# A Conformer and attention trunk on one core: two more channel blocks of the depthwise convolution on VectorE, pointwise weights' lower parts by accumulating DMA, GpSimd's arithmetic on other engines, and zero-padded lower rotary keys

## The chip, the cores and the metric

The kernel runs on one core of one Trainium2 chip. The metric is the device time of one execution in microseconds (us). A program is timed in several runs, and the median is given. One more execution is recorded by the hardware profiler; its span runs from the first instruction to the last one.

The core has five instruction queues: TensorE (PE, with its weight loads shown as PEld), VectorE (DVE), ScalarE (ACT), GpSimd (POOL) and SyncE (SP), which here only starts DMAs. POOL also starts DMAs, those that add into their destination.

## What is computed

Two layers of a trunk over 512 tokens with 1024 channels. Cut to what matters here:

```python
def conformer_conv(h, w_pw1, b_pw1, w_dw, b_dw, ln_g, ln_b, w_pw2, b_pw2):
    u = h @ w_pw1 + b_pw1
    a, gate = jnp.split(u, 2, axis=-1)
    u = a * jax.nn.sigmoid(gate)
    u = jnp.pad(u, ((0, 0), (CONV_WIDTH - 1, 0), (0, 0)))
    u = lax.conv_general_dilated(u, w_dw[:, None, :], ...) + b_dw
    u = jax.nn.silu(layer_norm(u, ln_g, ln_b))
    return u @ w_pw2 + b_pw2
...
        sc = (jnp.einsum('bqhd,bkhd->bhqk', qn, k_nope, ...)
              + jnp.einsum('bqhr,bkr->bhqk', qr, k_rope, ...)) * scale
...
def squared_relu_mlp(h, w1, w2):
    return jnp.square(jax.nn.relu(h @ w1)) @ w2
```

Layer 0 is the convolution module (31 taps for each channel) and a squared-ReLU MLP of width 4096. Layer 1 is attention with 8 heads, whose scores are the sum of a 128-wide product and a 64-wide rotary product that shares one key over all heads, and a second MLP.

## The kernel before, in words

Channels lie on the 128 partitions, tokens on the free axis, so each of the 8 channel blocks is a tile of 128 x 512. Every float32 product is made of three matmuls in a second 32-bit format (fp32r): each operand is split into an upper part (rounded to that format) and a lower part (what is left), and upper x upper, lower x upper and upper x lower are added in PSUM (`products_of`). A weight block of 128 x 1024 takes 24 matmuls.

**Weights** (`weight`). A block is loaded by SP into one of 3 `raw` buffers and split into one of 6 pairs `wh`, `wl`. For the blocks of the MLP (`ff1`, `ff2`) ACT writes the negated upper part into `wl` and the upper part into `wh`, and POOL starts a DMA that adds the block from memory onto `wl`. For all others ACT writes `wh` and DVE or POOL subtracts, whichever the planner takes (`VG`).

**The convolution module.** For each channel block c, pw1's blocks c and 8+c give the two halves; DVE multiplies each by the row norms (`za`, `zg`), ACT takes the sigmoid, DVE multiplies to `u`. The 31 taps are then done in one of two ways, given by a letter of `CONV`:

- V: `taps_vector`. ACT makes the first two taps, DVE the other 29, each one SCALAR_TENSOR_TENSOR of 128 x 482 to 510, into two accumulators, and adds these.
- T: `taps_tensor`. `u` is dealt through memory into one of three tiles `uu` (SP: one DMA `dealt<-big`, four `uu<-dealt`), nine weight tiles of 128 x 512 come from `cw`, and TensorE does 36 plain float32 matmuls of 128 x 128, whose results ACT (DVE for the last block) writes back in 16 pieces or more. `TAPS_AFTER` says behind which pw1 product a block's taps stand.

Before, two blocks are V and six are T. The layer norm over channels follows: an estimate of the mean (`K`, from blocks 0 and 1) is subtracted, sums and squares are added up, TensorE sums over partitions, and each block is normalised, put through SiLU and split for pw2.

**The MLP.** After each ff1 product, `z` = relu times norm on DVE, upper part of the square on ACT, the full square on POOL, their difference on DVE.

**Attention.** `scores` adds five matmuls into PSUM for each head and block of 128 queries. The fifth multiplies 64 rows only: `qr[rs]` with the lower half of the rotary key, `KR[1][rs]`.

**The order.** Nothing is issued where it stands in the code. All operations are recorded, and a planner (`Program`) with a cost for each kind of operation puts them into one order for each engine, chooses between VectorE and GpSimd where two ways are given (`binary`), gives out the buffers, and fills stretches where it expects TensorE to idle ahead of a new PSUM tile with matmuls on the identity that nothing reads (`mm<-ident`; 8 of them are 16 records of the trace). At run time each engine keeps that order and waits on semaphores. All instructions are therefore issued by one line of the code, line 556, and the trace is read by tiles, not by lines.

Of the kernel before, what the change touches and what calls it, by code (L numbers as in the profile page):

```python
# [15 lines left out]
T = 512  # L16
# [47 lines left out]

GAINS = {"dq": "mix_pre1", "dkv": "kvin_g", "kr": "kvin_g"}
# [40 lines left out]
CONV = "VTVTTTTT"  # L106
# [8 lines left out]
TAPS_AFTER = {1: 3, 3: 5, 4: 6, 5: 7, 6: 7}  # L115
# [112 lines left out]
class Program:  # L228
# [89 lines left out]
    def arrival(self, op, end, state):  # L318

        if "dma" not in op.method:  # L320
            return end
        n = max(_size(self.model(v)) for v in list(op.args) + list(op.kwargs.values()) if isinstance(v, View))
        state[0] = max(state[0], end + 650) + n * 1.42
        return state[0] + 850
# [235 lines left out]
def trunk(ctx: ExitStack, tc: tile.TileContext, xT, wts, vec, rope, cw, out):  # L560
# [25 lines left out]
    def pair():  # L586
        return big(F32R), big(F32R)
# [38 lines left out]
    def weight(key):  # L626

        while BLK[key] not in blocks:
            i = len(blocks)
            n = _cols[i]  # L630
            raw, hi, lo = nc.tile(RAW), nc.tile(WH, F32R), nc.tile(WL, F32R)
            step = 256 if i < 2 else n
            for o in range(0, n, step):
                nc.sync.dma_start(out=raw[:, o : o + step], in_=wts[i, :, o : o + step])
            if _names[i][0] in GAINS:
                for k in range(KT):
                    split_scaled(raw, v(GAINS[_names[i][0]], k), k * P, P, (hi, lo))
# [12 lines left out]
        return blocks[BLK[key]]  # L650
# [121 lines left out]
    def feed_forward(layer, X, r, F):  # L772

        for q in range(4):
# [4 lines left out]
            for m, (t0, n) in order:  # L779
# [8 lines left out]
                nc.gpsimd.tensor_tensor(out=zz[:, s], in0=z[:, s], in1=z[:, s], op=ALU.mult)  # L788
# [16 lines left out]
    def post_norm_groups(gen, F, on_half, g=None):  # L805
# [26 lines left out]
    for k in range(KT):  # L832
        a = (acc, part)[k % 2]
        sq = a if k < 2 else tmp()
        if k % 2:
            nc.scalar.activation(sq, h[k], AF.Square)
        else:
            nc.gpsimd.tensor_tensor(out=sq, in0=h[k], in1=h[k], op=ALU.mult)
        if k > 1:
            (nc.gpsimd, nc.vector)[k % 2].tensor_tensor(out=a, in0=a, in1=sq, op=ALU.add)  # L840
# [127 lines left out]
    for n, c in enumerate(LN_ORDER[:-1]):  # L968
        nc.vector.tensor_tensor(out=CO[c], in0=CO[c], in1=K, op=ALU.subtract)
        add_square(acc, CO[c], slice(0, T), n == 0, "gpsimd")  # L970
        if n == 0:
            xs = CO[c]
        else:
            xt = xs if n > 1 else big()
            nc.gpsimd.tensor_tensor(out=xt, in0=xs, in1=CO[c], op=ALU.add)
# [5 lines left out]
    for t0, n in (HA, HB):  # L981
# [13 lines left out]
        for c in range(KT):  # L995
            nc.binary(VG, out=CO[c][:, s], in0=CO[c][:, s], in1=dln[:, s], op=ALU.subtract)
# [57 lines left out]
    KR = pair()  # L1054
# [51 lines left out]
    for t in (HA, HB):  # L1106
# [3 lines left out]
        split(rotate(products(("kr",), XH, *t), t[1], s, r1), s, KR)  # L1110
# [39 lines left out]
    def scores(hd, half):  # L1150

        rs = slice(64 * (hd % 2), 64 * (hd % 2) + 64)
        PN[hd, half] = []
        kn, qn, qr = KN[hd], QN[hd], QR[hd]
        for i in (2 * half, 2 * half + 1):
# [5 lines left out]
            seq += [(qr[:, qs], KR[0][:, ks]), (qr[rs, qs], KR[1][rs, ks])]  # L1161
# [193 lines left out]
```

## Time and profile before

| | |
|---|---|
| median of 3 runs | 1167.62 us (1165.93 to 1168.73) |
| the profiled execution's own time | 1166.24 us |
| its span | 1164.5 us |
| TensorE busy | 1127.0 us, 97% of the span |
| ScalarE, VectorE, GpSimd busy | 621.3, 491.0, 400.7 us |
| mean granted TensorE clock | 0.994 |

How to read it: in a row of the timeline the first number is the start, the second the duration of the row's instructions together, both in us; a bracket at the end gives the idle time of that engine ahead of the row and what ended it. In a row of the stretches the numbers are the length, then the busy time of each engine with its count of instructions, the granted clock (PEclk), the mean busy share of the 16 DMA engines, and GB/s. A plain float32 matmul or filler has two records in the trace.

The stages, by the start of their first matmul: pw1 with the convolution from the start to 155.5 us, layer norm to 171.5, pw2 and the norms to about 250, the first MLP to 560, latent projections and norms to 660, attention to 780, output projection to 820, the second MLP to 1140, the end.

### The profile page before, as it was taken

The page shows a single profiled execution, that of the slowest core. Times are in us where ns is not written, and L with a number is a line of the kernel's source. Part 1 is how long each engine was busy: PE and PEld are TensorE (multiplying, and loading weights), DVE is VectorE, ACT ScalarE, POOL GpSimd, SP SyncE. Part 2 cuts the span into 40 slices and gives each one's busy share as a digit, 9 for nine tenths or more (in the row PEclk, how much of TensorE's full clock was granted, in tenths as well). Part 3 has the DMA queues.
Part 4 walks back from the last instruction along what each step waited for, and adds up shares of the span by engine and source line. Part 5 has one row for each costly group of instructions (what it writes and reads, how often), then busy time and mean ns, then how long its engine had stood idle before and what let it go on. Part 6 is the DMA issues. An engine that isn't in the chain of part 4 may idle for free.

```text
span 1164.5 us, 16571 instructions
## 1 busy us (share of the span) xinstructions
PE 1127.0 (97%) x6094; PEld 963.9 (83%) x6094; DVE 491.0 (42%) x1042; ACT 621.3 (53%) x1288; POOL 400.7 (34%) x423
## 2 busy tenths in 40 slices
PE   8998979999999999999989999999999999999997
PEld 6787979988888888888988877798888888888886
DVE  6898364671021121122698877428400211211215
ACT  4464748765544444454465867547644544444441
POOL 5573444452132132133333435145512312322322
PEclk9999989999999999999999999999999999999999
DMA  9556411669888888889210213245988987988842
GB/s 333 185 202 230 142 37 33 164 156 245 199 183 192 193 193 188 197 188 210 69 38 30 68 40 91 73 121 133 242 194 188 195 194 187 191 197 188 189 80 73
DMA packets 62865, 181.91 MB, mean 156 GB/s; under 512 B 7104, under 2 KB 15936, under 8 KB 62784
## 3 DMA queue, kind: packets, MB, share of 16 engines
q0 software_dynamic: 18432, 67.12, 34.2%
q1 hardware_dynamic: 43200, 112.69, 28.2%
q8 instruction: 48, 0.79, 0.3%
q10 hardware_dynamic: 1152, 1.05, 0.3%
q14 instruction: 33, 0.27, 0.1%
HBM read 177.15 MB, written 3.67 MB: 155 GB/s over the span
## 4 chain that ended last, share of the span: by engine, by line
PE 85%; DVE 9%; ACT 3%; issue 1%; DMA 0%; SPq 0%; POOL 0%; DVEq 0%
PE mm L556 82%; DVE big L556 5%; PE bc L556 3%; ACT big L556 3%; DVE tmp L556 2%; DVE stat L556 1%; DVE wl L556 1%; DMA h<-xT 0%; ACT tmp L556 0%; SPq L556 0%; DVE h L556 0%; ACT wh L556 0%; POOL h L556 0%; ACT wl L556 0%; DVEq L1351 0%
## 5 line engine op out<-in xcount | busy, mean ns | idle before, releaser
L556 PE MATMUL mm<-big,wh 128*128 128x512 f32 (+1 forms) x3304 | 897.9, 358 | 11.5 <-DVE big L556 9.1
L556 PEld LDWEIGHTS mm<-big,wh 128*128 128x128 f32 x3304 | 585.7, 189 | 108.7 <-DVE big L556 14.4
L556 PE MATMUL mm<-big,wl 128*128 128x512 f32 (+1 forms) x1652 | 586.1, 357 | 3.8 <-DVE wl L556 3.7
L556 PEld LDWEIGHTS mm<-big,wl 128*128 128x128 f32 x1652 | 311.5, 189 | 50.3 <-DVE wl L556 5.1
L556 ACT ACTIVATE wl<-raw 128x512 fp32r<-128x512 f32 x256 | 147.7, 624 | 321.7 <-issue 288.9
L556 ACT ACTIVATE wh<-raw 128x512 fp32r<-128x512 f32 (+2 forms) x348 | 196.1, 605 | 35.6 <-DMA raw<-wts 17.7
L556 POOL DMA_DIRECT2D wl<-wts x128 | 111.2, 869 | 284.0 <-ACT wl L556 268.7
L556 DVE TENSOR_TENSOR big<-mm,big 128x512 f32<-128x512 f32 (+3 forms) x102 | 60.6, 599 | 206.2 <-PE mm L556 191.7
L556 DVE SCALAR_TENSOR_TENSOR tmp<-mm,big 128x512 f32<-128x512 f32 (+1 forms) x72 | 44.8, 630 | 241.6 <-PE mm L556 240.6
L556 POOL TENSOR_TENSOR tmp<-tmp 128x512 f32<-128x512 f32 (+1 forms) x72 | 69.8, 972 | 195.2 <-DVE tmp L556 190.1
L556 POOL TENSOR_TENSOR wl<-raw,wh 128x512 fp32r<-128x512 f32 (+2 forms) x67 | 91.0, 1377 | 96.7 <-ACT wh L556 88.4
L556 DVE TENSOR_TENSOR big<-tmp,big 128x512 fp32r<-128x512 f32 (+1 forms) x86 | 54.4, 639 | 87.2 <-POOL tmp L556 43.7
L556 ACT ACTIVATE big<-mm 128x512 fp32r<-128x512 f32 (+5 forms) x102 | 51.1, 504 | 44.6 <-PE mm L556 43.8
L556 POOL TENSOR_TENSOR big<-big,tmp 128x256 f32<-128x256 f32 (+1 forms) x40 | 42.6, 1066 | 60.6 <-ACT tmp L556 56.6
L556 POOL TENSOR_TENSOR h<-h,tmp 128x256 f32<-128x256 f32 x56 | 44.0, 846 | 47.8 <-DVE tmp L556 47.8
L556 POOL TENSOR_TENSOR big<-big,big 128x256 f32<-128x256 f32 (+2 forms) x34 | 37.6, 1109 | 64.7 <-ACT big L556 38.4
L556 DVE SCALAR_TENSOR_TENSOR big<-big,vt,big 128x510 f32<-128x510 f32 (+28 forms) x58 | 57.7, 1050 | 0.0
L556 PE MATMUL mm<-big,big 128*128 128x256 f32 (+7 forms) x256 | 56.1, 344 | 0.0
L556 ACT ACTIVATE big<-mm,vt 32x128 f32<-32x128 f32 (+1 forms) x96 | 46.2, 482 | 13.6 <-PE mm L556 12.5
L556 DVE TENSOR_TENSOR big<-big,tmp 128x256 f32<-128x256 f32 (+1 forms) x65 | 36.2, 560 | 37.1 <-ACT tmp L556 24.5
L556 PEld LDWEIGHTS mm<-big,big 128*128 128x128 f32 (+1 forms) x256 | 39.6, 188 | 12.9 <-issue 7.8
L556 PEld LDWEIGHTS mm<-uu,big 128*128 128x128 f32 x432 | 48.8, 192 | 0.3
(78 smaller groups left out, 706.7 us busy)
## 6 DMA issues: line engine op xcount, KB each, us to landing
raw<-wts SPq DMA_DIRECT2D x164, 512.0 KB, 6.1
wl<-wts POOLq DMA_DIRECT2D x128, 512.0 KB, 6.7
big<-cw SPq DMA_DIRECT2D x54, 256.0 KB, 5.0
raw<-wts SPq DMA_DIRECT2D x12, 192.0 KB, 2.3
h<-xT SPq DMA_DIRECT2D x8, 256.0 KB, 4.5
raw<-wts SPq DMA_DIRECT2D x16, 128.0 KB, 2.6
dealt<-big SPq DMA_DIRECT2D x6, 256.0 KB, 2.1
uu<-dealt SPq DMA_DIRECT2D x24, 64.0 KB, 3.3
```

The costliest lines, as they stand in the source:

```text
L556: return f(*args, **kwargs)
```

## The change

- `CONV` becomes `VVTVTVTT`: blocks 0, 1, 3 and 5 on VectorE, 2, 4, 6 and 7 on TensorE; `TAPS_AFTER` follows.
- `weight`: pw1 and pw2 blocks from the fifth on get their lower part like the MLP's, by ACT and an accumulating DMA; the first four, and `dq` and the like as before, by VectorE alone. The weights of attention keep the choice of two engines.
- GpSimd's element-wise work in the start, the layer norm, the sums of squares and the MLP's square goes to VectorE or ScalarE. The residual additions, the rotary rotation and the splits of attention's weights stay.
- The lower part of the rotary key becomes two tiles of 128 rows, one for even and one for odd heads, with zeros in the other half, so that the fifth matmul of `scores` has 128 rows.
- The planner's model gives an accumulating DMA 2.03 times the time of a plain one.

```diff
-CONV = "VTVTTTTT"
+CONV = "VVTVTVTT"
...
-TAPS_AFTER = {1: 3, 3: 5, 4: 6, 5: 7, 6: 7}
+TAPS_AFTER = {2: 4, 4: 6, 6: 7}
...
+        slow = 2.03 if "accum_op" in op.kwargs else 1.0
+        state[0] = max(state[0], end + 650) + n * 1.42 * slow
+        return state[0] + 850 * slow
...
-            elif _names[i][0] in ("ff1", "ff2"):
+            elif i >= 4 and _names[i][0] in LO_BY_DMA:
...
-                engines = VG
+                engines = VG if _names[i][0] in ATT else ("vector",)
...
-                nc.gpsimd.tensor_tensor(out=zz[:, s], in0=z[:, s], in1=z[:, s], op=ALU.mult)
+                nc.scalar.activation(zz[:, s], z[:, s], AF.Square)
...
-                add_square(accs[0], F[m], s, m == 0, "gpsimd" if m < 6 else "vector")
+                add_square(accs[0], F[m], s, m == 0, "vector")
...
-        if k % 2:
-            nc.scalar.activation(sq, h[k], AF.Square)
-        else:
-            nc.gpsimd.tensor_tensor(out=sq, in0=h[k], in1=h[k], op=ALU.mult)
+        nc.scalar.activation(sq, h[k], AF.Square)
...
-            nc.binary(VG, out=CO[c][:, s], in0=CO[c][:, s], in1=dln[:, s], op=ALU.subtract)
+            nc.binary(("vector",), out=CO[c][:, s], in0=CO[c][:, s], in1=dln[:, s], op=ALU.subtract)
...
-        split(rotate(products(("kr",), XH, *t), t[1], s, r1), s, KR)
+        kr = rotate(products(("kr",), XH, *t), t[1], s, r1)
+        nc.scalar.activation(KR[:, s], kr[:, s], AF.Copy)
+        for j in range(2):
+            rows = slice(64 * j, 64 * j + 64)
+            nc.vector.tensor_tensor(
+                out=KL[j][rows, s], in0=kr[rows, s], in1=KR[rows, s].bitcast(F32), op=ALU.subtract
+            )
...
-            seq += [(qr[:, qs], KR[0][:, ks]), (qr[rs, qs], KR[1][rs, ks])]
+            seq += [(qr[:, qs], KR[:, ks]), (qr[:, qs], KL[hd % 2][:, ks])]
```

The planner makes new orders of all this. Counted over the whole program, TensorE's taps go from 216 matmuls to 144, its fillers from 28 to 96, GpSimd's element-wise operations from 278 to 108, its DMAs from 128 to 148, VectorE's taps from 58 to 116, ScalarE's instructions from 1266 to 1354 and SP's DMAs of `cw` from 54 to 36.

TensorE at the end of pw1, before: the last matmul of pw1 (`wh15` is the sixteenth block's upper part) and what follows it. `uu00` is the dealt tile of block 5, and two more T blocks follow it.

```order
L556 MATMUL mm21_1224<-big15_336,wh15_811 128x512
L556 MATMUL mm22_1268<-uu00_98,big59_689 128x128 x4
L556 MATMUL mm22_1268<-uu00_98,big60_704 128x128 x4
L556 MATMUL mm22_1268<-uu00_98,big61_714 128x128
L556 MATMUL mm23_1287<-uu00_98,big61_714 128x128 x3
```

The same place after; `uu20` is block 6's dealt tile, and only block 7's taps follow it.

```order
L560 MATMUL mm19_1115<-big15_278,wh15_858 128x512
L560 MATMUL mm20_1288<-ident0_96 128x128 x65
L560 MATMUL mm20_1288<-uu20_113,big53_770 128x128 x4
L560 MATMUL mm20_1288<-uu20_113,big54_777 128x128 x4
L560 MATMUL mm20_1288<-uu20_113,big55_785 128x128
```

Two blocks of taps stand behind pw1's end in place of three, and 65 fillers ahead of the first of them.

VectorE around the last `u` (block 7's, the row with 128x128x4), before; `mm21` is pw1's last product, and the rows with `mm26` are the write-back of block 7's taps.

```order
L556 TENSOR_TENSOR big33_613<-big33_613,big58_1021 128x512
L556 TENSOR_TENSOR tmp31_1226<-mm20_1169,big16_410 128x512
L556 TENSOR_TENSOR tmp29_1271<-mm21_1224,big16_410 128x512
L556 SCALAR_TENSOR_TENSOR big90_1292<-tmp31_1226,vt0_94,tmp30_1281 128x128x4
L556 TENSOR_TENSOR big79_1317<-big79_1317,big58_1021 128x512
L556 SCALAR_TENSOR_TENSOR big93_1418<-mm26_1398,vt0_94,big58_1021 32x128 x4
```

And after, where `mm19` is pw1's last product and `big50`, `big51` are the accumulators of V block 5.

```order
L560 SCALAR_TENSOR_TENSOR big50_1009<-big49_999,vt0_94,big50_1009 128x484
L560 TENSOR_TENSOR tmp29_1249<-mm19_1115,big16_378 128x512
L560 TENSOR_TENSOR big76_1254<-big29_416,big32_510 128x512
L560 SCALAR_TENSOR_TENSOR big51_605<-big49_999,vt0_94,big51_605 128x483
L560 SCALAR_TENSOR_TENSOR big74_1260<-tmp31_1127,vt0_94,tmp30_1256 128x128x4
L560 SCALAR_TENSOR_TENSOR big50_1009<-big49_999,vt0_94,big50_1009 128x482
L560 TENSOR_TENSOR big75_1147<-big75_1147,tmp32_1003 128x512
L560 TENSOR_TENSOR big76_1254<-big76_1254,big47_895 128x512
```

Block 7's `u` now stands among block 5's last taps, behind 115 taps in all, and the sums for the layer norm stand on VectorE right behind it.

More of the change, by code (lines that the diff above doesn't have):

```diff
@@ L63 @@
 _cols, _names = [], []
+LO_BY_DMA = ("ff1", "ff2", "pw1", "pw2")
+ATT = ("uq", "uqr", "uk", "uv", "wo")
 GAINS = {"dq": "mix_pre1", "dkv": "kvin_g", "kr": "kvin_g"}
@@ L322, in arrival @@
         n = max(_size(self.model(v)) for v in list(op.args) + list(op.kwargs.values()) if isinstance(v, View))
-        state[0] = max(state[0], end + 650) + n * 1.42
-        return state[0] + 850
+        slow = 2.03 if "accum_op" in op.kwargs else 1.0
+        state[0] = max(state[0], end + 650) + n * 1.42 * slow
+        return state[0] + 850 * slow
     def due(self, start):
@@ L834, in trunk @@
         sq = a if k < 2 else tmp()
-        if k % 2:
-            nc.scalar.activation(sq, h[k], AF.Square)
-        else:
-            nc.gpsimd.tensor_tensor(out=sq, in0=h[k], in1=h[k], op=ALU.mult)
+        nc.scalar.activation(sq, h[k], AF.Square)
         if k > 1:
-            (nc.gpsimd, nc.vector)[k % 2].tensor_tensor(out=a, in0=a, in1=sq, op=ALU.add)
+            nc.vector.tensor_tensor(out=a, in0=a, in1=sq, op=ALU.add)
     nc.vector.tensor_tensor(out=acc, in0=acc, in1=part, op=ALU.add)
@@ L969, in trunk @@
         nc.vector.tensor_tensor(out=CO[c], in0=CO[c], in1=K, op=ALU.subtract)
-        add_square(acc, CO[c], slice(0, T), n == 0, "gpsimd")
+        add_square(acc, CO[c], slice(0, T), n == 0, "vector")
         if n == 0:
@@ L974, in trunk @@
             xt = xs if n > 1 else big()
-            nc.gpsimd.tensor_tensor(out=xt, in0=xs, in1=CO[c], op=ALU.add)
+            nc.vector.tensor_tensor(out=xt, in0=xs, in1=CO[c], op=ALU.add)
             xs = xt
@@ L1002, in trunk @@
                     nc.scalar.activation(rln[:, s], rlnp[:, :n], AF.Copy)
-                nc.binary(VG, out=xn[:, s], in0=CO[c][:, s], in1=rln[:, s], op=ALU.mult)
+                nc.binary(("vector",), out=xn[:, s], in0=CO[c][:, s], in1=rln[:, s], op=ALU.mult)
             for out_ in (Y[c][0], y):
                 nc.scalar.activation(out_[:, s], xn[:, s], AF.Silu, scale=v("ln_g", c), bias=v("ln_b", c))
-            nc.binary(VG, out=Y[c][1][:, s], in0=y[:, s], in1=Y[c][0][:, s].bitcast(F32), op=ALU.subtract)
+            nc.binary(("vector",), out=Y[c][1][:, s], in0=y[:, s], in1=Y[c][0][:, s].bitcast(F32), op=ALU.subtract)
     def skewed(name, X, halves=False):
@@ L1053, in trunk @@
     CQ = [pair() for _ in range(3)]
-    KR = pair()
+    KR, KL = big(F32R), [big(F32R) for _ in range(2)]
+    for j in range(2):
+        nc.gpsimd.memset(KL[j][64 - 64 * j : 128 - 64 * j].bitcast(F32), 0.0)
     def latent(name, g, dst, t, dim):
@@ L1109, in trunk @@
         latent("dkv", "kv_g", CKV, t, 256)
-        split(rotate(products(("kr",), XH, *t), t[1], s, r1), s, KR)
+        kr = rotate(products(("kr",), XH, *t), t[1], s, r1)
+        nc.scalar.activation(KR[:, s], kr[:, s], AF.Copy)
+        for j in range(2):
+            rows = slice(64 * j, 64 * j + 64)
+            nc.vector.tensor_tensor(
+                out=KL[j][rows, s], in0=kr[rows, s], in1=KR[rows, s].bitcast(F32), op=ALU.subtract
+            )
     O = [pair() for _ in range(KT)]
@@ L1150, in scores @@
     def scores(hd, half):
-        rs = slice(64 * (hd % 2), 64 * (hd % 2) + 64)
         PN[hd, half] = []
```

## The prediction

> **What bounds the kernel now.** The chain of work that ended last, by engine:
>
> ```profile
> PE 85%; DVE 9%; ACT 3%; issue 1%; DMA 0%; SPq 0%; POOL 0%; DVEq 0%
> ```
>
> GpSimd and the DMAs, where most of the change lies, hold nothing of the end. So the second view is the stages one by one (in each row length, then PE, PEld, DVE, ACT, POOL busy):
>
> ```profile
> 0.00:33.30 33.30, 27.60 (x126) 21.42 (x127) 21.56 (x29) 15.96 (x31) 17.25 (x27) 1.00 0.92 337
> 33.30:131.20 97.90, 94.75 (x526) 81.85 (x525) 82.48 (x90) 54.12 (x99) 48.88 (x31) 1.00 0.62 205
> 131.20:155.50 24.30, 24.30 (x217) 24.08 (x215) 5.42 (x8) 19.43 (x38) 14.54 (x12) 1.00 0.15 45
> 155.50:171.50 16.00, 10.70 (x60) 9.63 (x59) 12.60 (x45) 3.83 (x9) 6.80 (x7) 0.79 0.10 33
> 250.00:560.00 310.00, 309.64 (x1362) 254.28 (x1361) 61.32 (x101) 148.03 (x278) 83.65 (x94) 1.00 0.87 199
> 660.00:780.00 120.00, 119.36 (x672) 98.96 (x673) 67.05 (x169) 73.78 (x167) 41.75 (x37) 1.00 0.24 73
> ```
>
> TensorE has no gap in the MLP (309.64/1362 = 0.227 us per matmul), next to none in attention, and little in pw1. VectorE is the second engine of pw1: 82.5 of 97.9 us. So I look at two places: what the convolution costs TensorE and how close VectorE follows, and what a 64-row matmul costs in attention.
>
> **The taps on TensorE.** Its timeline in pw1:
>
> ```profile
> 26.69 1.95 PE L556 MATMUL mm<-ident 128*128 128x128 f32 x16
> 28.40 0.48 PE L556 MATMUL mm<-big,wh 128*128 128x512 f32 x1
> ...
> 59.51 8.20 PE L556 MATMUL mm<-uu,big 128*128 128x128 f32 x72
> 67.46 0.48 PE L556 MATMUL mm<-big,wh 128*128 128x512 f32 x1
> ...
> 103.23 0.74 PE L556 MATMUL bc<-tmp,meanmat 128*128 128x512 f32 x2 [3.15 <-ACT tmp L556]
> ...
> 131.23 24.28 PE L556 MATMUL mm<-uu,big 128*128 128x128 f32 x216
> ```
>
> A T block takes 67.46 - 59.51 = 7.95 us, a filler (28.40 - 26.69)/8 = 0.21. Two T blocks go: -15.9 us. The order after has 68 fillers more (96 against 28): +14.5 us. They are real instructions, which TensorE carries out whether it would have idled or not, so almost all that the taps free is given back. The wait of 3.15 us is for the mean estimate, which needed block 1's T taps; both its blocks are V now and, by the sum below, done some us ahead of TensorE's need: -3.2 (bounds -3.2 and 0).
>
> TensorE's end of pw1 moves from 131.2 to 131.2 - 7.95 (two T blocks ahead of it in place of three) - 3.2 + 0.6 (three fillers more at the start) = 120.7; then 65 fillers (13.9) to 134.6, block 6 to 142.5, block 7 to about 151 against 155.5: **-4.6 us**, if block 7's dealt tile is there at 143.
>
> **Is it?** That hangs on VectorE, whose 29 taps a block double from 58 to 116:
>
> ```profile
> L556 DVE SCALAR_TENSOR_TENSOR big<-big,vt,big 128x510 f32<-128x510 f32 (+28 forms) x58 | 57.7, 1050 | 0.0
> ...
> 37.98 0.75 DVE L556 SCALAR_TENSOR_TENSOR big<-tmp,vt,tmp 128x512 f32<-128x512 f32 x1 [1.53 <-ACT tmp L556]
> ...
> 39.25 0.68 DVE L556 TENSOR_TENSOR tmp<-mm,big 128x512 f32<-128x512 f32 x1
> ...
> 53.96 3.46 DVE L556 SCALAR_TENSOR_TENSOR big<-big,vt,big 128x501 f32<-128x501 f32 x2
> ...
> 97.81 5.24 DVE L556 SCALAR_TENSOR_TENSOR big<-big,vt,big 128x501 f32<-128x501 f32 x8
> ```
>
> GpSimd beside them, and the stretch of the eight fast taps:
>
> ```profile
> 50.50 6.37 POOL L556 TENSOR_TENSOR wl<-raw,wh 128x512 fp32r<-128x512 f32 x4 [3.81 <-ACT wh L556]
> ...
> 97.80:103.00 5.20, 2.29 (x10) 1.50 (x8) 5.20 (x9) 5.06 (x11) 0.00 (x0) 1.00 0.95 363
> ```
>
> With GpSimd subtracting (50.5 to 56.9) a tap takes 1.73 us, with GpSimd idle 5.24/8 = 0.65, even with ScalarE full and the DMAs at 0.95. After, GpSimd does no arithmetic in this stage. From the first `u` (38.0) to block 7's `u` the order has 115 taps (74.8 us), 21 plain operations (at 0.68 at most, 14.3) and six `u` of about 1 us: 95 us, so 133 if VectorE never waits. Then the deal:
>
> ```profile
> 133.27 1.59 DVE L556 SCALAR_TENSOR_TENSOR big<-tmp,vt,tmp 128x512 f32<-128x512 f32 x1 [1.15 <-ACT tmp L556]
> ...
> 136.92 1.74 SPq L556 DMA_DIRECT2D uu<-dealt  x4
> ...
> uu<-dealt SPq DMA_DIRECT2D x24, 64.0 KB, 3.3
> ```
>
> From `u`'s end at 134.9 to the last landing (138.7 + 3.3 = 142.0) took 7 us; 133 + 1 + 7 = 141 against TensorE's 142.5. It fits, by some 2 us; an earlier start of VectorE, whose operations no longer share with GpSimd from 10 us on, may add to it. I book nothing. Block 6's tile is queued on SP behind six loads of `cw`; 13.9 us of fillers hide that.
>
> **Weights.** For twelve pw1 and eight pw2 blocks the subtraction becomes two ACT passes, a DMA start on GpSimd, and a DMA:
>
> ```profile
> L556 ACT ACTIVATE wl<-raw 128x512 fp32r<-128x512 f32 x256 | 147.7, 624 | 321.7 <-issue 288.9 <-PE mm L556 18.3 <-DMA raw<-wts 13.7
> ...
> L556 POOL DMA_DIRECT2D wl<-wts x128 | 111.2, 869 | 284.0 <-ACT wl L556 268.7 <-issue 6.7 <-PE bc L556 6.1
> ...
> DMA to landing us min/median/max: 5.2/6.7/12.0
> ```
>
> That is 2 x 0.62 + 0.87 + 6.7 = 8.8 us (14.1 at the slowest landing; the last row is of the first MLP), hidden where blocks are five ahead of 24 x 0.227 = 5.5 us each. They are not at the start: block 4 comes first by this way. SP has six fewer `cw` tiles ahead of its load (6 x 0.26 MB at 337 GB/s, 4.7 us), which covers about half; the other half falls into the 5.7 us for which TensorE idled in 0 to 33.3 anyhow. I take 0, bounds -4 and +4. In the MLP ScalarE takes the square too:
>
> ```profile
> L556 POOL TENSOR_TENSOR tmp<-tmp 128x512 f32<-128x512 f32 x56 | 57.8, 1033 | 189.1 <-DVE tmp L556 189.1
> ...
> L556 ACT ACTIVATE big<-tmp 128x512 fp32r<-128x512 f32 x56 | 34.5, 616 | 0.5 <-DVE tmp L556 0.3
> ```
>
> Two of 0.62 in a row against 1.03 beside 0.62: the chain grows by 0.2 us, and the first ff2 product needs the last of them 21 matmuls (4.8 us) in; ScalarE goes from 148 to about 168 of 310 us. +0.5, bounds 0 and +3. Layer norm and pw2's start lose waits on GpSimd but get all of VectorE's work in one queue: -1, bounds -3 and +2. The square sums go to VectorE in stages where it is busy 20% to 50%: 0.
>
> **The padded key.** Weight loads around two 64-row matmuls, and all of these loads:
>
> ```profile
> 658.52 0.77 PEld L556 LDWEIGHTS mm<-big,big 128*128 128x128 f32 x4
> 659.54 0.18 PEld L556 LDWEIGHTS mm<-big,big 64*128 64x128 f32 x1 [0.25 <-issue]
> 659.91 0.76 PEld L556 LDWEIGHTS mm<-big,big 128*128 128x128 f32 x4 [0.19 <-issue]
> 661.04 0.18 PEld L556 LDWEIGHTS mm<-big,big 64*128 64x128 f32 x1 [0.36 <-issue]
> 661.47 1.76 PEld L556 LDWEIGHTS mm<-big,big 128*128 128x128 f32 x12 [0.25 <-issue]
> ...
> L556 PEld LDWEIGHTS mm<-big,big 64*128 64x128 f32 x32 | 5.8, 183 | 6.5 <-issue 5.1
> ```
>
> Ten loads take 661.47 - 658.52 = 2.95 us. Without the gaps five stand 0.19 apart (0.77 - 0.19 over 3) and five 0.23: 2.1 us. So a visit costs 0.43, and 32 cost 13.6; the floor is the idle time ahead of the loads alone, 6.5. The load behind a visit comes somewhat early, which takes back part: 11. The padded one is a plain 128-row matmul; the two tiles cost VectorE one operation more per half. Since TensorE is busy 119.4 of 120 us here and VectorE 67, nearly all should reach the end: **-10**, bounds -13.6 and -6.5. The Trainium skill, "TensorE: Matmul & The Clock Gate", section "Why this matters for your kernels", says that a single matmul with K of 32 takes the same time as one with 128. By it this term would be 0; the gaps of 0.19 to 0.36 us on both sides speak against it.
>
> **Sum.** -4.6 + 0 + 0.5 - 1 - 10 = -15.1. The profiled execution took 1166.24 (span 1164.5 and 1.7 around it), 1.4 under the median of 1167.62; I carry the difference over to the median: 1167.6 - 15.1 = **1152.5**. With the bounds drawn at random rather than all one way, 1145 to 1160.
>
> **The rivals.**
>
> *Starting a DMA hinders the taps.* No row has GpSimd starting DMAs beside uninterrupted taps. If each of the 15 starts in pw1 stops VectorE for its 0.87 us, block 7's `u` comes 13 us late, of which 2 are spare: 1152.5 + 11 = 1163. The Trainium skill, "GPSIMD Engine Reference", section "Key points", has GpSimd contend with VectorE instructions that read two inputs from SBUF, which the 1.73 us tap bears out; its page "DMA: Bandwidth & Descriptors", section "SWDGE vs HWDGE vs iDMA", says that GpSimd writes such a DMA's descriptors into SBUF. 0.12.
>
> *Slower: taps stay slow.* If what slows a tap is not GpSimd's arithmetic alone, and the mean stays at 1.05 us, 115 taps take 46 us more, and with 2 spare the end is 44 later: about 1196. It decides from a mean of (2 + 15.1)/115 = 0.15 above 0.65, that is 0.80 us. For it: most taps of before are slow. Against: the eight at 0.65 with all else busy. 0.10.
>
> *Late weights.* An MLP block uses 0.87 x 5.46 = 4.7 us of all DMA engines, of which the plain load, at 337 GB/s and 0.92, is 1.4; an accumulation is thus 3.3. Twelve to sixteen add 40 to 53 us, eighteen `cw` tiles less take 13 off the 61 (0.62 x 97.9) in pw1: 88 to 101 in a stage of 87. At the upper end TensorE would wait 14 us: 1166.5, no change. For it: that sum. Against: four of the sixteen are pw2's and not needed yet. 0.08.
>
> *The padding gives nothing*, by the rule above, or because softmax's chain takes the place of TensorE: 1162.5. 0.07.
>
> *That the change doesn't do what it says* is so in part: GpSimd keeps 108 operations, but none in pw1.
>
> **Chances.** 0.63 for the forecast; about 0.2% (2.3 us) is what a measurement can tell from no change. Faster: forecast, DMA starts, padding and half of late weights, 0.86; same: 0.04, late weights' other half; slower: 0.10. The range leaves out the slower case, the end of late weights and some of the forecast's tails: 1143 to 1164.
>
> **What would show it.** Right: block 7's taps end near 151; taps take 0.65 us with GpSimd's wait-free rows gone; no 64-row load; attention some 10 us shorter; the MLP unchanged. Wrong: a TensorE wait on `wl` in pw1, taps over 0.8 us, a wait behind the 65 fillers, VectorE or ScalarE ending TensorE's waits in attention. If the fillers end long after block 6's tile has landed, they cost what they were to hide.

## The result and the profile after

| | before | after |
|---|---|---|
| median | 1167.2 us (1165.9 to 1168.7) | 1140.7 us (1140.1 to 1142.7) |
| the profiled execution's own time, and its span | 1166.2, 1164.5 us | 1140.1, 1137.9 us |
| TensorE busy | 1127.0 us | 1108.9 us |
| GpSimd busy | 400.7 us | 233.9 us |

The ratio is 0.9775 (95% interval 0.9758 to 0.9792): 26.5 us faster, where 15.1 were forecast and the range ended at 1143. The direction and the place of most terms are as forecast; 11 us are not in the sum.

The chain that ended last still runs over TensorE, by engine:

```profile
PE 85%; DVE 8%; DMA 3%; ACT 2%; issue 1%; SPq 0%; POOL 0%; DVEq 0%; ACTq 0%; POOLq 0%
```

So the stages have to be compared. I cut both traces at the same seven events of TensorE: the last tap, pw2's first product, the last statistics matmul ahead of the first MLP, the first sum of the norm behind that MLP, the first and the last matmul that has both operands in `big` (attention), and the last matmul. Some of the MLP's first products run ahead of the third event, so part of them falls on either side of that cut; where it matters I add the two stages. Columns: length, then busy time of PE, PEld, DVE, ACT and POOL, the granted clock, DMA share, GB/s. Before:

```profile
0.00:155.20 155.20, 146.35 (x865) 127.23 (x866) 109.17 (x127) 89.51 (x168) 80.66 (x68) 1.00 0.61 208
155.20:168.70 13.50, 9.07 (x49) 8.19 (x48) 10.38 (x36) 2.75 (x7) 6.07 (x6) 0.75 0.12 39
168.70:252.10 83.40, 76.94 (x613) 74.85 (x611) 54.31 (x134) 61.25 (x140) 40.59 (x51) 0.98 0.40 94
252.10:573.30 321.20, 321.20 (x1461) 265.97 (x1459) 66.08 (x108) 150.62 (x287) 85.05 (x96) 1.00 0.84 194
573.30:645.60 72.30, 66.67 (x501) 62.43 (x501) 64.11 (x208) 46.71 (x135) 25.34 (x30) 1.00 0.12 35
645.60:746.40 100.80, 100.16 (x539) 79.66 (x538) 73.00 (x195) 72.57 (x168) 40.98 (x35) 1.00 0.21 63
746.40:1156.10 409.70, 406.33 (x2079) 345.49 (x2078) 109.35 (x226) 197.92 (x385) 119.28 (x135) 1.00 0.74 169
```

After:

```profile
0.00:150.60 150.60, 145.11 (x861) 127.27 (x862) 122.31 (x201) 98.17 (x181) 17.27 (x35) 1.00 0.84 243
150.60:165.50 14.90, 8.75 (x49) 8.12 (x47) 12.19 (x40) 2.12 (x6) 0.00 (x0) 0.77 0.00 0
165.50:240.20 74.70, 73.16 (x608) 72.44 (x607) 51.54 (x155) 62.51 (x145) 20.42 (x26) 1.00 0.49 114
240.20:561.20 321.00, 321.00 (x1465) 266.51 (x1464) 65.23 (x111) 167.89 (x323) 50.84 (x61) 1.00 0.82 195
561.20:629.70 68.50, 65.39 (x498) 61.66 (x497) 65.00 (x210) 47.34 (x136) 26.15 (x31) 1.00 0.12 38
629.70:722.40 92.70, 90.56 (x542) 79.28 (x541) 71.03 (x195) 69.74 (x167) 43.33 (x36) 1.00 0.23 73
722.40:1129.80 407.40, 404.65 (x2076) 344.76 (x2075) 112.25 (x238) 214.97 (x421) 73.05 (x86) 1.00 0.71 168
```

The differences of the lengths are -4.6 (convolution), +1.4 (layer norm), **-8.7 (pw2 and the norms behind it)**, -0.2 (first MLP), -3.8 (norms and latents), -8.1 (attention), -2.3 (the rest): -26.3. In the row of pw2 TensorE's idle time fell from 6.5 us to 1.5 and the clock rose from 0.98 to 1.00. The 0.98 is one stretch of 3.4 us at half clock, which begins at two waits of TensorE, 1.68 us up to 174.9 and 0.48 us up to 176.9:

```profile
176.60:180.00 3.40, 3.15 (x14) 3.15 (x15) 2.08 (x4) 3.40 (x9) 3.40 (x5) 0.50 0.00 0
```

Nothing else was out by as much.

TensorE's timeline at the end of the convolution is the one that was forecast (fillers to 134.6, block 6 to 142.5, block 7 to about 151):

```profile
119.44 0.40 PE L560 MATMUL mm<-big,wh 128*128 128x512 f32 x1
119.68 14.68 PE L560 MATMUL mm<-ident 128*128 128x128 f32 x130
134.19 8.20 PE L560 MATMUL mm<-uu,big 128*128 128x128 f32 x72
142.23 0.61 PE L560 MATMUL mm<-ident 128*128 128x128 f32 x4
142.68 8.20 PE L560 MATMUL mm<-uu,big 128*128 128x128 f32 x72
150.72 0.50 PE L560 MATMUL bc<-col,big 128*128 128x128 f32 x3
```

So are the taps on VectorE, in the page's group of them:

```profile
L560 DVE SCALAR_TENSOR_TENSOR big<-big,vt,big 128x487 f32<-128x487 f32 (+25 forms) x116 | 76.5, 731 | 0.9 <-ACT big L560 0.9
```

76.5/116 = 0.66 us each, against 0.65 forecast (the mean of 731 ns counts the overlap of neighbours twice). And so are attention's weight loads, 22 in one row without a gap, where before the two 64-row visits stood:

```profile
640.75 3.91 PEld L560 LDWEIGHTS mm<-big,big 128*128 128x128 f32 x22
644.70 0.48 PEld L560 LDWEIGHTS bc<-ident,big 128*128 128x128 f32 x3
```

From the first of them to the `bc` load behind are 3.95 us. Before, the same 22 began at 658.52, and the `bc` load behind them was this one:

```profile
663.28 0.69 PEld L556 LDWEIGHTS bc<-ident,big 128*128 128x128 f32 x5
```

That is 4.76 us, 0.40 more for each of the two visits, and 13 for 32.

What TensorE waited for from pw2 to the first MLP, before and after (us in total, times, longest):

```profile
PE mm L556 <- DVE big L556: 5.0, 6, 1.7
PE bc L556 <- DVE stat L556: 0.8, 2, 0.5
PE mm L556 <- ACT big L556: 0.5, 1, 0.5
```

```profile
PE mm L560 <- DVE big L560: 1.5, 3, 0.8
```

VectorE ended most of these waits. Its largest wait in this stage before, and GpSimd's rows (busy, mean ns, then idle ahead and what ended it):

```profile
L556 DVE TENSOR_TENSOR big<-big,tmp 128x256 f32<-128x256 f32 x18 | 10.3, 572 | 13.5 <-POOL big L556 12.3 <-ACT tmp L556 1.1
...
L556 POOL TENSOR_TENSOR big<-big,tmp 128x256 f32<-128x256 f32 x10 | 8.2, 820 | 10.3 <-ACT tmp L556 10.0
L556 POOL TENSOR_TENSOR big<-big,big 128x256 f32<-128x256 f32 x6 | 5.1, 855 | 2.4 <-ACT big L556 2.4
```

After, VectorE does them all, and faster each:

```profile
L560 DVE TENSOR_TENSOR big<-big,tmp 128x256 f32<-128x256 f32 x28 | 12.4, 458 | 16.5 <-ACT tmp L560 16.1
...
L560 DVE TENSOR_TENSOR big<-big,big 128x256 f32<-128x256 f32 x10 | 4.0, 417 | 0.0
```

A step of 0.82 to 0.86 us on GpSimd is one of 0.42 to 0.46 on VectorE. The 12.3 us for which VectorE waited on GpSimd are gone, but they are not the gain. They are a single wait, and TensorE was busy all through it (the second row is the same stretch; VectorE now waits as long there on ScalarE, 16.1 us):

```profile
208.92 0.42 DVE L556 TENSOR_TENSOR big<-big,tmp 128x256 f32<-128x256 f32 x1 [12.29 <-POOL big L556]
196.60:208.90 12.30, 12.30 (x105) 12.30 (x105) 0.03 (x1) 8.10 (x19) 6.81 (x8) 1.00 0.67 176
```

Nor does the chain that ended last hold a GpSimd step in this stage before. Beside TensorE it holds VectorE and ScalarE:

```profile
by line: PE mm L556 61.6%; DVE big L556 14.2%; DVE tmp L556 6.5%; issue 4.6%; PE bc L556 4.6%; DVE stat L556 4.2%; ACT big L556 2.4%; ACT tmp L556 1.2%; ACT wl L556 0.8%; DVEq L556 0.1%
```

What GpSimd's arithmetic does to that chain is seen in VectorE's own steps. Of its 52 additions, subtractions and multiplications of two 128x256 tiles in this stage before, the 20 that lie beside arithmetic on GpSimd took 0.76 us in the mean and the other 32 took 0.42. After, 3 lie beside it and 67 do not. So VectorE carries out 21 instructions more (155 against 134) and yet is busy for 51.5 us in place of 54.3; only 2.6 us of that are weight splits that it no longer has. This gives theory A; whether GpSimd's steps cost more by being slow themselves or by slowing VectorE's, no run separates, and the chain speaks for the second.

### The profile page after: what moved, and what is told of

It reads as the page before. It is cut to its first block, busy times and chain, and to the rows that moved or that the text cites. A ratio compares the mean times of both kernels' runs of the same rounds, so it can differ in the third digit from the quotient of the medians.

```text
span 1137.9 us, 16389 instructions
## 1 busy us (share of the span) xinstructions
PE 1108.9 (97%) x6086; PEld 960.1 (84%) x6086; DVE 504.1 (44%) x1158; ACT 662.7 (58%) x1376; POOL 233.9 (21%) x277
## 3 DMA queue, kind: packets, MB, share of 16 engines
q10 hardware_dynamic: 1152, 1.05, 0.3%
## 4 chain that ended last, share of the span: by engine, by line
PE 85%; DVE 8%; DMA 3%; ACT 2%; issue 1%; SPq 0%; POOL 0%; DVEq 0%; ACTq 0%; POOLq 0%
PE mm L560 82%; DVE big L560 5%; PE bc L560 3%; ACT big L560 2%; DVE tmp L560 2%; DMA wl<-wts 1%; DVE stat L560 1%; DMA big<-cw 1%; DVE wl L560 1%; DMA vt<-vec 1%; DMA raw<-wts 0%; SPq L560 0%; ACT tmp L560 0%; ACT wh L560 0%; ACT wl L560 0%
## 5 line engine op out<-in xcount | busy, mean ns | idle before, releaser
L560 ACT ACTIVATE wl<-raw 128x512 fp32r<-128x512 f32 x296 | 171.1, 623 | 286.3 <-issue 191.6
L560 POOL DMA_DIRECT2D wl<-wts x148 | 128.2, 866 | 734.9 <-ACT wl L560 658.2
L560 DVE SCALAR_TENSOR_TENSOR big<-big,vt,big 128x487 f32<-128x487 f32 (+25 forms) x116 | 76.5, 731 | 0.9 <-ACT big L560 0.9
L560 ACT ACTIVATE tmp<-big 128x256 f32<-128x256 f32 (+2 forms) x61 | 28.2, 473 | 48.1 <-DVE big L560 47.8
L560 POOL TENSOR_TENSOR wl<-raw,wh 128x512 fp32r<-128x512 f32 (+2 forms) x34 | 38.5, 1147 | 61.0 <-ACT wh L560 60.7
L560 PE MATMUL mm<-big,big 128*128 128x256 f32 (+3 forms) x256 | 46.3, 325 | 0.0
L560 ACT ACTIVATE big<-tmp 128x512 fp32r<-128x512 f32 (+1 forms) x72 | 41.1, 570 | 6.3 <-DVE tmp L560 6.3
L560 PEld LDWEIGHTS mm<-big,big 128*128 128x128 f32 x256 | 38.9, 189 | 3.3 <-DVE big L560 0.2
L560 ACT ACTIVATE tmp<-tmp 128x512 f32<-128x512 f32 (+1 forms) x72 | 40.9, 569 | 0.0
L560 ACT ACTIVATE big<-mm,vt 32x128 f32<-32x128 f32 (+1 forms) x64 | 30.4, 479 | 10.8 <-PE mm L560 10.2
L560 DVE TENSOR_TENSOR big<-big,big 128x512 f32<-128x512 f32 (+4 forms) x52 | 28.9, 576 | 13.8 <-ACT big L560 13.7
```

The costliest lines, as they stand in the source:

```text
L560: return f(*args, **kwargs)
```

## The experiments

**Theory A:** the missing gain lies in GpSimd's arithmetic of the layer norm and the sums of squares, which stood in or beside the chain that feeds TensorE from pw2 on. **Theory B:** it lies in pw2's weights, whose splits VectorE no longer does. **Theory C:** it follows from what happens ahead of pw2. From the third group on there is a fourth, **theory L:** part of it belongs to no edit, but to the order that the planner happened to give.

### Parts of the change alone, on the kernel before

**Layer norm and sums of squares on VectorE** (the other parts as before):

```diff
-add_square(accs[0], F[m], s, m == 0, "gpsimd" if m < 6 else "vector")
+add_square(accs[0], F[m], s, m == 0, "vector")
-add_square(acc, CO[c], slice(0, T), n == 0, "gpsimd")
+add_square(acc, CO[c], slice(0, T), n == 0, "vector")
-nc.gpsimd.tensor_tensor(out=xt, in0=xs, in1=CO[c], op=ALU.add)
+nc.vector.tensor_tensor(out=xt, in0=xs, in1=CO[c], op=ALU.add)
-nc.binary(VG, out=CO[c][:, s], in0=CO[c][:, s], in1=dln[:, s], op=ALU.subtract)
+nc.binary(("vector",), out=CO[c][:, s], in0=CO[c][:, s], in1=dln[:, s], op=ALU.subtract)
```

(and the multiplication and the lower part behind the last line likewise)

> The kernel before, with only GpSimd's arithmetic in the layer norm and in the sums of squares ahead of the norms moved to VectorE (weights, convolution, the MLP's square and the key as before). Theory A (this arithmetic was what TensorE waited for from the layer norm to the first MLP, 7.3 us of the 26.5, and a little at the next norm): 6 to 9 us faster. Theory B (pw2's lower parts by DMA freed VectorE there) and theory C (what happens ahead of it, pw1's earlier end, brings the loads of pw2 earlier): 0 to 1 us faster, as the prediction booked.

1153.9 us: 12.7 faster (ratio 0.9887, 0.9872 to 0.9902). More than A had said; B falls, since the weights are as before. Its stage of pw2 takes 76.1 us against 83.4, but its convolution also ends 5.1 sooner, so C is still open.

**The padded key alone** (the key's lines of the diff):

> The kernel before, with only the padded lower key. The prediction's term: 10 us faster, between 6.5 and 13.6. The stages of the two traces from the end of the first MLP to the end of the output projection differ by 13.3 us: if all of that is the key, 13 faster. By the rule that 64 rows cost what 128 cost: 0.

1163.5 us: 3.1 faster (0.9959 to 0.9987), below my lower bound. Yet attention itself is 7.0 shorter (93.8 against 100.8). The gain was lost elsewhere: the norms and latents ahead of it took 75.8 us against 72.3, in a stage to which the edit adds only a few small operations. The profiled execution was, at 1168.2, the longest of its runs, so its later stages can't be set against the median.

**The weights alone** (lower parts by DMA, other splits outside attention on VectorE, the planner's price):

> The kernel before, with only the weights' change: lower parts of pw1's and pw2's blocks from the fifth on by ScalarE and an accumulating DMA, the other splits outside attention by VectorE alone, and the planner's price for such a DMA. Theory A: pw1 gains at most the wait for the mean of 3.2 us, pw2 nothing: 0 to 4 us faster. Theory B: pw2 and the norms behind it gain another 5: 5 to 9 us faster.

1191.4 us: 24.8 slower (1.0185 to 1.0221). Neither theory had that. TensorE's timeline shows where:

```profile
136.44 8.20 PE L557 MATMUL mm<-uu,big 128*128 128x128 f32 x72
144.48 19.82 PE L557 MATMUL mm<-ident 128*128 128x128 f32 x176
164.13 16.24 PE L557 MATMUL mm<-uu,big 128*128 128x128 f32 x144
```

88 fillers stand ahead of the last two blocks' taps: the planner expected their dealt tiles late, and late they were, with the eight loads started from 145.2 to 154.0 us and 2.9 to 9.2 us more to land. With six T blocks there are 54 tiles of `cw` beside the accumulating DMAs, and the DMAs are busy at 0.96 to the end of pw1 (0.62 before):

```profile
33.30:134.60 101.30, 97.53 (x529) 83.97 (x530) 57.01 (x85) 64.42 (x122) 19.74 (x21) 0.98 0.96 266
```

pw1 itself ends 3.4 us later; the rest is the tiles.

**The convolution alone** (`CONV` and `TAPS_AFTER`):

> The kernel before, with only the convolution's change: four blocks each on VectorE and TensorE, while GpSimd still subtracts beside them. If GpSimd's arithmetic is what makes a tap 1.05 us in the mean, the 115 taps ahead of the last block's product take some 46 us more than at 0.65, and this kernel is 25 to 45 us slower than before. If taps are not hindered by it, some 5 us faster.

1196.8 us: 30.3 slower (1.0231 to 1.0269). GpSimd still subtracts, and the taps take 98.6/116 = 0.85 us:

```profile
L556 DVE SCALAR_TENSOR_TENSOR big<-big,vt,big 128x505 f32<-128x505 f32 (+25 forms) x116 | 98.6, 911 | 0.1
```

That is above the 0.80 from which the prediction's slower rival was to decide, but here GpSimd does subtract beside the taps, which it no longer does in the changed kernel. 116 taps at 0.19 more are 22 of the 30 us. The layer norm can't begin before VectorE is done with the last block, and TensorE carries out 177 fillers of 0.11 us a record meanwhile:

```profile
141.24 8.20 PE L556 MATMUL mm<-uu,big 128*128 128x128 f32 x72
149.28 39.69 PE L556 MATMUL bc<-ident 128*128 128x128 f32 x354
```

So two parts that cost 25 and 30 us alone are in the change that gains 26. Whether each is there for the other is tried below.

### Where the parts' gain and loss lie

**The sums of squares alone** (the first pair of lines above):

> The kernel before, with only the sums of squares of the sandwich norms (behind pw2, the MLPs and attention) moved from GpSimd to VectorE; the layer norm stays as it was. Norms and layer norm together gave 12.7 us. If the chains of the sandwich norms are what mattered: 6 to 11 us faster. If it was the layer norm and its sums beside the taps: 0 to 4 us faster. The prediction had booked 0 for this.

1168.3 us: 1.5 slower (1.0004 to 1.0024). By the total A falls for the sandwich norms. By the stage it seems to stand: pw2 and the norms take 78.8 us against 83.4. But 1.3 of these 4.6 us stand in the first MLP now, and with the two stages added, 401.3 us is what other orders of the kernel before take as well (401.4 to 404.6, from the table below). A gain of the sums of squares by themselves is not shown. The rest was lost in stages that the edit doesn't touch or hardly: the convolution (+1.6), attention (+1.6), and behind it (+1.7). This was the first sign of theory L.

**Layer norm, sums of squares and the key together:**

> The kernel before, with the layer norm's and the norms' arithmetic on VectorE and the padded key. If the parts add up: 12.7 and 3.1, 15.8 us faster. If the key's gain in attention (7.0 us in its own trace) was given back at the norms before and behind attention, by GpSimd's sums there: 19 to 21 us faster.

1152.2 us: 14.7 faster (0.9860 to 0.9893), 1.7 beyond the norms alone. Attention is 6.2 shorter than with the norms alone (95.8 against 102.0), the convolution 4.7 longer (154.8 against 150.1), though no edit between the two kernels is there. My reading that GpSimd's sums ate the key's gain falls. The stage of pw2 takes 76.1 us as with the norms alone, although here the convolution ends at 154.8, near the 155.2 of before: that speaks against theory C.

**Fewer fillers, on the changed kernel:**

```diff
-for _ in range(int((now - since - 60) / (FILL if pace else 2 * FILL))):
+for _ in range(min(45, int((now - since - 60) / (FILL if pace else 2 * FILL)))):
```

> The changed kernel with 45 in place of 65 fillers ahead of block 6's taps. Block 6's dealt tile has landed at 129 at the latest, block 7's at about 139, and with the 65 the taps of block 6 began at 134 and those of block 7 at 142.7. If the fillers cost what they were to hide: 3.5 us faster than the changed kernel. If the layer norm waits for VectorE and not for the taps: no difference.

1137.3 us, 3.4 below the changed kernel: 65 fillers were more than block 6's tile needed. The row of fillers ends 4.7 us sooner, and no wait follows it. The stage of pw2 begins 5.0 us sooner and still takes 74.7, so theory C is out (the stretch behind attention takes 1.8 more):

```profile
119.41 10.21 PE L560 MATMUL mm<-ident 128*128 128x128 f32 x90
129.45 8.20 PE L560 MATMUL mm<-uu,big 128*128 128x128 f32 x72
```

**The residual additions on VectorE too, on the changed kernel** (`engine = nc.vector`):

> The changed kernel with the residual additions, GpSimd's last arithmetic in the norms, on VectorE too. If a GpSimd step of 0.9 us in the chain ahead of a norm costs TensorE time, as in theory A: 2 to 6 us faster than the changed kernel. If the chains have slack by now (TensorE waits only 1.5 us from pw2 to the first MLP): within 1 us.

1140.2 us, no difference in the total. In the stage of pw2 TensorE now has no idle time at all:

```profile
164.50:236.80 72.30, 72.30 (x604) 71.97 (x603) 50.11 (x169) 62.99 (x145) 8.63 (x10) 1.00 0.53 126
```

It is 2.4 shorter than in the changed kernel, but 1.0 of this stands in the first MLP (322.0 against 321.0), and the latents (72.3 against 68.5) take back the rest.

### Parts taken back, and the order by itself

**The three steps of the normalisation back to VectorE or GpSimd, on the changed kernel** (`nc.binary(VG, ...)`):

> The changed kernel, with only the three steps of the layer norm's normalisation (subtract mean, multiply, lower part) given back to the choice between VectorE and GpSimd. If these are what the prediction undersized (it booked 1 us for the layer norm and pw2's start; the traces differ by 7.2 us from pw2's first product to the first MLP): 5 to 8 us slower than the changed kernel, with half clock or waits back in pw2. If that gain came from the weights or from another order alone: within 2 us.

1145.8 us, 5.1 slower than the changed kernel (ratios to before 0.9801 to 0.9830 and 0.9758 to 0.9792). Its row of the stage has the clock of 0.98 back:

```profile
166.70:245.10 78.40, 75.09 (x610) 74.09 (x608) 53.27 (x137) 62.43 (x146) 32.09 (x40) 0.98 0.47 109
```

3.7 of the 5.1 us are in this stage; the others are 1.6 in the convolution and 2.1 in attention. VectorE never waits for GpSimd in it, but 17 of its 59 two-input steps lie beside GpSimd's arithmetic again, with 0.77 us each against 0.42 for the others.

**The 64-row key back, on the changed kernel:**

> The changed kernel with the lower rotary key of 64 rows as before. By the prediction's term and by the length of attention (100.8 us before, 92.7 after): 8 to 10 us slower than the changed kernel. By the two pairs of experiments with and without the padding on the kernel before (3.1 and 2.0 us): 2 to 3 slower.

1149.5 us, 8.8 slower (0.9835 to 0.9865). Every other stage is within 0.9 us of the changed kernel's, and attention is 101.7 us against 92.7: the term is 9.0 in this pair of orders. In the two experiments on the kernel before, attention itself was 7.0 and 6.2 us shorter; the totals are lower because the new order lost time in other stages.

**The convolution and the weights together, on the kernel before:**

> The kernel before with the convolution's and the weights' change together, which cost 30 and 25 us each alone; layer norm, norms, square and key as before. If each is the cover for the other's cost (fewer taps' weights for the accumulating DMAs, no GpSimd subtraction beside the taps on VectorE): 0 to 8 us faster than before. If the costs are separate: 40 to 55 slower.

1177.9 us: 10.8 slower (1.0066 to 1.0108), a fifth of the 55 of the two alone, but no gain. The fall from 55 shows that they cover most of each other's cost. What is left is, in its trace, 2.5 us in the convolution and 2.4 in the layer norm, where GpSimd's sums for the layer norm still lie beside the taps, and 8.4 in attention, where the granted clock is 0.94 with no wait over 1.6 us. That clock is two stretches at half clock, 3.4 us from 692.2 on and this one, right behind a wait of 1.58 us:

```profile
651.60:661.80 10.20, 10.20 (x27) 6.97 (x27) 4.71 (x18) 3.74 (x11) 1.72 (x2) 0.52 0.11 35
```

Half of 13.6 us is 6.8, an estimate of what they cost. Why the clock stayed low for 10.2 us with TensorE busy is open.

**The same instructions in another order, on the kernel before:**

```diff
-return 68 + rate * n + 62 * few
+return 72 + rate * n + 62 * few
```

> The kernel before with the planner's price for a VectorE instruction raised from 68 to 72 ns plus length: the same instructions, in another order. If the planner's order alone moves time between stages: stage boundaries move by 1 to 5 us, the total by up to 4 either way. If the order is of no account: all within 0.5 us.

1158.3 us: **8.8 faster** (0.9913 to 0.9952) without an edit of the work, more than the 4 that I had allowed. Its stage of pw2:

```profile
166.10:247.20 81.10, 77.46 (x617) 75.69 (x616) 52.20 (x129) 62.41 (x142) 43.69 (x55) 0.98 0.44 100
```

It gains 2 us each in the convolution, in pw2, in the latents and behind attention. So how much of the 26.5 is this?

### The spread of the order

**The planner's price at 64 and at 76, before; at 64 and at 72, after:**

> The kernel before, only the planner's price for a VectorE instruction lowered from 68 to 64 ns plus length: the same instructions in another order. With 72 it was 8.8 us faster. Theory L (the order of the kernel before was an unlucky one, and some 8 of the 26.5 us are luck): 4 to 10 us faster than before. Theory E (the edits made all of it): within 3 us of before, 72 being the exception.

> The kernel before with 76 ns in the planner: as with 64. Theory L: 4 to 10 us faster than before. Theory E: within 3.

> The changed kernel with 64 ns in place of 68 in the planner: the same instructions in another order. If the changed kernel's order was a lucky one: 3 to 8 us slower than the changed kernel. If the changed kernel depends little on the order, since fewer chains run over GpSimd: within 2.

> The changed kernel with 72 ns in the planner: as with 64. Lucky order: 3 to 8 us slower than the changed kernel. Little dependence: within 2.

The medians are 1165.7 and 1162.8 for before, 1142.9 and 1139.2 for after. Theory L as I put it (4 to 10 faster) holds for one of two; theory E's limit of 3 for the other. On the changed kernel the two orders are 2.2 us slower and 1.5 faster, so its order was not the lucky one. Before, four orders lie between 1158.3 and 1167.2 with a mean of 1163.5, and the given one is the slowest; after, three lie between 1139.2 and 1142.9 with a mean of 1140.9, and the given one is in the middle. Of the 26.5 us, 1167.2 - 1163.5 = 3.7 are thus the order of before, and 22.6 the edits. The lengths of the stages, in us, cut as above (64, 68, 72, 76 before; 64, 68, 72 after):

| stage | before | after | difference of means | forecast |
|---|---|---|---|---|
| convolution | 155.2, 155.2, 152.8, 158.8 | 149.6, 150.6, 150.1 | -5.4 | -4.6 |
| layer norm | 13.1, 13.5, 13.3, 13.3 | 14.7, 14.9, 13.7 | +1.1 | -1, with the next |
| pw2, norms | 81.8, 83.4, 81.1, 82.6 | 75.3, 74.7, 73.6 | -7.7 | |
| first MLP | 321.5, 321.2, 320.3, 319.8 | 321.0, 321.0, 320.7 | +0.2 | +0.5 for both MLPs |
| norms, latents | 67.8, 72.3, 70.4, 70.1 | 71.4, 68.5, 68.1 | -0.8 | 0 |
| attention | 104.7, 100.8, 101.5, 103.8 | 93.4, 92.7, 96.6 | -8.5 | -10 |
| the rest | 410.5, 409.7, 407.7, 406.7 | 407.2, 407.4, 406.3 | -1.7 | |

The latents' 3.8 us, which the two traces alone would have given to an edit, are inside the spread of the orders (67.8 to 72.3 before, 68.1 to 71.4 after).

**pw2's weights split as before, on the changed kernel:**

```diff
-LO_BY_DMA = ("ff1", "ff2", "pw1", "pw2")
+LO_BY_DMA = ("ff1", "ff2", "pw1")
-engines = VG if _names[i][0] in ATT else ("vector",)
+engines = VG if _names[i][0] in ATT + ("pw2",) else ("vector",)
```

> The changed kernel with the lower parts of pw2's weights split as before by VectorE or GpSimd in place of the accumulating DMA. From pw2's first product to the first MLP the four orders of before take 81.1 to 83.4 us and the three of after 73.6 to 75.3; giving back the layer norm's steps returned 3.7. If the other 4 us of that stage are the weights': 3 to 5 us slower than the changed kernel. If they are not: within 2.

1137.1 us, 3.6 *below* the changed kernel (ratios 0.9726 to 0.9766 and 0.9758 to 0.9792, which overlap a little). The stage of pw2 stays at 75.0, so B is out. The gain is ahead of it:

```profile
119.05 8.20 PE L560 MATMUL mm<-uu,big 128*128 128x128 f32 x72
127.09 4.18 PE L560 MATMUL mm<-ident 128*128 128x128 f32 x36
131.11 8.20 PE L560 MATMUL mm<-uu,big 128*128 128x128 f32 x72
139.15 5.75 PE L560 MATMUL bc<-ident 128*128 128x128 f32 x50
```

Block 6's taps follow pw1 at once. Without the first pw2 blocks' accumulating DMAs in pw1 the tile is dealt sooner (its loads start at 108.4 us in place of 115.0), and the convolution ends 11.6 us earlier, at 139.0; the layer norm, for which VectorE is now late, takes 6.3 of it back. A total of 3.6 us is no more than what another order moved the changed kernel by (3.7), so it is not shown that the weights make it.

**45 fillers and 72 ns together:**

> The changed kernel with 45 in place of 65 fillers and with 72 ns in the planner. If the two gains (3.4 and 1.5 us beside 1140.7) add up: 1135.8 us. If the order shifts what the fillers freed: 1137 to 1139.

1134.8 us (ratio 0.9727, 0.9712 to 0.9743): 5.9 below the changed kernel, the fastest here. The two gains add up and 1 us more. Block 7's taps now wait 1.3 us for their tile, so 45 is about as few as this order bears:

```profile
137.21 0.61 PE L560 MATMUL mm<-ident 128*128 128x128 f32 x4
139.15 8.30 PE L560 MATMUL mm<-uu,big 128*128 128x128 f32 x72 [1.33 <-DMA uu<-dealt]
```

## Why the prediction was wrong

**Convolution, -4.6: right.** -4.6 in the two traces, -5.4 over the orders. That the taps would take 0.65, that fillers give back what the T blocks freed, and that block 7's tile would be there at 143 (by the trace it had landed at 139) all came so. That the figure fits to the tenth is luck: over the four orders of before this stage lies between 152.8 and 158.8. The warning about fillers that end after the tile has landed came true too, for 3.4 us.

**Padded key, -10 (-13.6 to -6.5): right.** -8.1 in the traces, -8.5 over the orders, 8.8 when it is taken back. Part of the 13 us that the loads save is idle time now, 2.1 us of attention. The Trainium skill's rule in "TensorE: Matmul & The Clock Gate", section "Why this matters for your kernels", by which the term was 0, does not carry over to single 64-row matmuls that stand between 128-row ones: these runs have 0.40 us for each.

**First MLP and start: right** (+0.2; no wait on ScalarE's square appears).

**"Layer norm and pw2's start lose waits on GpSimd but get all of VectorE's work in one queue: -1, bounds -3 and +2", and "the square sums go to VectorE in stages where it is busy 20% to 50%: 0": wrong, and the main error.** Together with the layer norm's +1.1 these stages gave 6.6 us over the orders, 7.3 in the two traces. What went wrong is the cost that I set against the waits, "all of VectorE's work in one queue". The queue hardly got longer: with the layer norm and the sums of squares alone on VectorE it carries out 157 instructions in this stage in place of 134 and is busy for 55.8 us in place of 54.3. A step moved from GpSimd takes about half the time, and VectorE's own steps fall from 0.76 to 0.42 us when GpSimd does no arithmetic beside them. I had read just this off the taps (1.73 against 0.65 us) and used it in pw1 alone. And the size was not worked out from a row. The rows were at hand: TensorE was idle for 83.4 - 76.9 = 6.5 us of the stage and lost 1.7 more to 3.4 us at half clock, so some 8 could go. The "20% to 50%" does not hold for this stage either, in which ten of GpSimd's sums of squares stand: VectorE is busy for 54.3 of its 83.4 us, 65%. The share that is busy says whether an engine has room, not how long the chain is. The idle time of TensorE in this stage goes with GpSimd's work in it:

| kernel | GpSimd busy | TensorE idle | length |
|---|---|---|---|
| before | 40.6 | 6.5 | 83.4 |
| before, three other orders | 43.7 to 44.8 | 3.6 to 6.2 | 81.1 to 82.6 |
| sums of squares moved | 35.0 | 5.5 | 78.8 |
| after, normalisation moved back | 32.1 | 3.3 | 78.4 |
| layer norm and sums moved | 23.7 | 2.1 | 76.1 |
| after | 20.4 | 1.5 | 74.7 |
| after, two other orders | 20.5, 21.9 | 1.8, 0.6 | 75.3, 73.6 |
| after, residuals moved too | 8.6 | 0.0 | 72.3 |

With about the same work on GpSimd the orders of before differ by up to 2.9 us in idle time, so neighbouring rows can't be told apart; the kernels of before and of after can. The normalisation's three steps carry 3.7 us (the kernel with them back). What the sums of squares carry is open: pw2 and the first MLP together fall by 7.5 us in the means, and the sums alone gave 1.6 of it, at the edge of the spread.

**A term that was not in the sum: the order.** A change that alters any operation makes the planner order the whole program anew, and that alone moved before by 8.9 us between four orders and after by 3.7 between three. I carried one execution of one order to the median and gave the order no bounds; it was the slowest of four, by 3.7 against their mean. This, beside the two parts that need each other, is why the parts alone don't add up. Four orders are few: their standard deviation is 3.9, so the mean is uncertain by some 2 us.

**The rivals.** DMA starts that hinder the taps: out, with taps of 0.66 us beside the 17 instructions that GpSimd has in pw1. The Trainium skill, "SBUF — State Buffer", section "Who interferes with whom", says that a VectorE instruction with two inputs in SBUF contends with a GpSimd instruction that reads SBUF; 0.65 with GpSimd idle, 0.66 with it only starting DMAs and 0.85 with it subtracting agree. Slow taps: out, since it put the 1.05 us down to something other than GpSimd's arithmetic, and without that arithmetic a tap takes 0.66. That slow taps do cost time is shown by the convolution's part alone (0.85 us a tap, 30 us slower); the weights' part took GpSimd's subtraction away from them. Late weights: the DMAs were nearly full, by the row of pw1 (0.98),

```profile
33.30:119.60 86.30, 83.96 (x446) 71.63 (x445) 84.06 (x131) 55.33 (x102) 13.94 (x17) 1.00 0.98 264
```

but TensorE waited 0.7 us in all for a `wl` by DMA. What the full DMAs delayed was the dealt tiles, hidden from the waits by fillers; the kernel with pw2's weights split as before, whose block 6 needs no fillers, is 3.6 us faster, but in another order.

In sum, of the 11.2 us between forecast and traces 6.3 are the layer norm's and the norms' steps (7.3 against 1), 3.8 the latents, which the orders make likely to be no edit's, and 3.0 the MLPs and what lies behind attention; attention itself gave 1.9 less. By the means over the orders 22.6 - 15.1 = 7.5 us are left, and 5.6 of them are the layer norm's and the norms' steps. What carries the -1.7 behind attention, by the means, is open.

## What to carry to other kernels

For a chain of small steps that feeds TensorE, read TensorE's idle time and granted clock in that stage as about the most that shortening it can give (8.2 us here, against the 8.7 that came). One step back, look at how long the feeding engine's steps take with and without another engine beside them; a long wait of that engine counts only where TensorE is idle too. The busy share of the engine that takes the work over says little of it. Where a planner orders the program, time a few orders of the same work before a difference of under 1% is given to an edit, and take a part back from the full change rather than adding it alone. Dummy matmuls turn a wait into busy time: where a row of them stands, look up when the tile behind it landed.

## What the runs showed of the hardware beyond that

- Two plausible parts of one change cost 25 and 30 us alone and 10.8 together: GpSimd's subtraction slowed VectorE's taps from 0.66 to 0.85 us, and the accumulating DMAs beside 54 `cw` tiles held the dealt tiles back, for which 19.8 us of fillers stood in.
- TensorE's granted clock was 0.75 and 0.77 in the layer norm of before and after, with waits of some us in it, but it also fell to a half at much shorter ones: for 3.4 us at waits of 1.68 and 0.48 us (before, in pw2), for 3.4 us behind waits of 0.58 and 1.03 us (the changed kernel with 72 ns, from 627.6 on), and for 10.2 us behind one of 1.58 us (convolution and weights, in attention). Not every such wait does it: one of 1.51 us in pw2 before, up to 225.8, has no such stretch behind it.
